# Norm means and prompt steps in the scores' spare PSUM columns, and two attention maps combined with the first map's sum left in

## The chip, the core and the metric

The kernel runs on one core of a Trainium2 chip. The metric is device time of one execution in microseconds. The engines are TensorE (PE; its weight loads are listed as PEld), VectorE (DVE), ScalarE (ACT), GpSimd (POOL) and SyncE (SP), whose queue issues the DMAs. Each engine works through its own list of instructions in order. TensorE reads SBUF and writes PSUM, which has eight banks of 512 float32 columns on 128 partitions; VectorE and ScalarE read PSUM.

## What is computed

One step of a two-layer model on 128 prompt tokens and 1024 sample tokens, width 1024. Each layer makes an input projection, differential attention in four heads, a Fourier branch and a gated spatial branch, and an output projection. The change is in the attention alone. Of the reference:

```python
def _diff_attention(q, k, v, lam, subln_w, lam_init):
    s = jnp.einsum('bhqmd,bhkmd->bhmqk', q, k) * (HEAD_DIM ** -0.5)
    p = jax.nn.softmax(s, axis=-1)
    a = p[:, :, 0] - lam * p[:, :, 1]
    o = jnp.einsum('bhqk,bhke->bhqe', a, v)
    o = o * lax.rsqrt(jnp.mean(jnp.square(o), axis=-1, keepdims=True) + RMS_EPS) * subln_w * (1.0 - lam_init)
    return o
```

The sample tokens attend to 1152 keys (1024 of their own and 128 cached), in blocks of 128 queries; the prompt's 128 tokens attend to themselves. Each head has two maps, m = 0 and 1, and the second is subtracted with the weight lam.

## The kernel before

An attention stage (one per layer) runs 4 heads of 8 blocks of 128 queries. For a block, `score` (lines 632 to 644) multiplies queries and keys of one map into a PSUM tile `S` of three banks, 384 columns of the 512 in each; VectorE takes the negated maximum `nm` (line 640), and ScalarE the exponential `P` with its row sum `zz` (line 642). That is done for both maps. `softmax_diff` (lines 580 to 585) combines them: VectorE takes reciprocals `rz`, GpSimd multiplies the second map by its reciprocal and by minus lam (line 584), and VectorE multiplies the first and adds (line 585). One block later `transpose` (lines 646 to 656) turns the result by nine TensorE transposes into a tile `T`; ScalarE copies it out (line 655) and VectorE takes the remainder `lo` (line 656). For every second block `values` (lines 658 to 665) multiplies by the values into `pv`, squares it on ScalarE, and `finish_o` (lines 592 to 604) takes the mean of the squares over a head's 128 dimensions by a matmul with a matrix of 1/128 (line 594), copies it with epsilon added on ScalarE (`msq`, line 598), and forms the norm by logarithm, exponential and GpSimd products on the gate `gs`.

`S`, `T` and `pv` share the tag `S`: two buffers of three banks each, used in turn, so that each matmul group waits until the group two before it has been read. The other two banks (tag `mm`) serve the projections, whose matmuls (`z`, line 386, and `zt`, lines 401 and 406) fill TensorE between the attention steps. `prompt` (lines 670 to 693) does the prompt's own attention in steps that are stepped on between the others (`side.fill`, paced by `PACE`), with tiles of tag `mm`: two scores `sp`, a transpose `atp`, and the product with its mean, `pvp`.

TensorE's order is the order of the code (`manual_schedule`, line 1059); `attention` (lines 695 to 757) yields between its steps and the loop then issues filler of `FILL[h] * SHARE[step]` ns, 1500 or 1600 per unit in the first three heads and 2950 in the fourth. The order of the other engines is chosen by the scheduler of the framework, from priorities. SBUF tiles share buffers by tag, as the lists `X_TAGS` say: `msq` and `sq` are two of the names in a tag of three buffers, and the prompt's `Pp` is in another.

```python
with tc.manual_schedule(engines={mybir.EngineType.PE}):
    for n, (h, step) in enumerate(attention(l, fill)):
        fill.fill(FILL[h] * SHARE[step])
        if h >= MHEAD:
            extra.fill(MFILL)
```

Of the kernel before, what the change touches and what calls it, by code (L numbers as in the profile page):

```python
# [10 lines left out]
F32 = mybir.dt.float32  # L11
# [20 lines left out]
PACE = 2  # L32
# [19 lines left out]
X_TAGS = {"wr": ("wraw", "woraw", "wada", "tabr", "mr", "ba"), "z": ("zz", "sh", "gt", "vT", "gmt", "gmg", "fot", "vs", "bd", "pqp", "ws", "kc", "vc", "Pp", "modacc"), "Q": ("Q", "bdr", "wsr", "h32"),  # L52
          "sq": ("sq", "wft", "dftp", "msq", "bds", "cb")}
# [9 lines left out]
def backbone_step(ctx, tc, xs, xp, cT, w_ada, b_ada, w_in, w_out, ckT, cv, lamv, wf, wsT, bsT,  # L63
# [60 lines left out]
    mix_d = [dr.tile([128, NT, 6, 128], F32, name=f"mix_{l}") for l in range(L)]  # L124
    neglam = cp.tile([128, L], F32, name="neglam")
# [466 lines left out]
    def finish_o(l, o, ms, sq, n, gs, sl):  # L592

        pe.matmul(ms, lhsT=onesm, rhs=sq[:, :n], start=True, stop=True)
        dve.scalar_tensor_tensor(gs[:, sl], o, subs[:, l:l + 1], gs[:, sl], op0=ALU.mult, op1=ALU.mult)

        m = tX([128, 256], "msq")[:, :n]
        act.activation(m, ms, AF.Identity, bias=epsr)
# [8 lines left out]
    class Head:  # L607
        def __init__(self, l, h):
            self.l, self.h = l, h
            (self.K, self.kp), (self.qr, self.qp) = (res.pop((n, l, h)) for n in "kq")  # L610
# [21 lines left out]
        def score(self, Q, i, m, zz):  # L632
# [3 lines left out]
            for e, q in enumerate((Q[:, m, ql], qlo[i % 2][:, m])):  # L636
                for n in range(3):
                    pe.matmul(S[:, n, :CH], lhsT=q, rhs=K[:, m, n * CH:(n + 1) * CH], start=e == 0, stop=e == 1)  # L638
            nm = small([128, 1], "nm", 4)
# [3 lines left out]
                           accum_out=zz[:, m:m + 1])  # L643
            return P

# [12 lines left out]
        def values(self, p):  # L658
            pv = psS((128, 2, 256), "pv")
            for kt in range(NT):  # L660
                for e, (a, b) in enumerate(((0, 0), (0, 1), (1, 0))):
                    pe.matmul(pv[:, 0, :], lhsT=self.V[:, a, kt, :], rhs=self.A[:, b, kt, :],  # L662
                              start=kt == 0 and e == 0, stop=kt == 8 and e == 2)
            sq = square_o(pv[:, 0], 256)
            return lambda: finish_o(self.l, pv[:, 0], pv[:, 1], sq, 256, self.gs, slice(p * 256, (p + 1) * 256))
# [4 lines left out]
        def prompt(self):  # L670

            l = self.l
            nm = small([128, 2], "nmp", 2)
            zz = small([128, 2], "zzp", 2)
            P = tX([128, 2, 128], "Pp")
            for m in range(2):
                S = psM((128, 128), "sp")
# [476 lines left out]
```

## Time and profile before

| | us |
|---|---|
| median of 3 runs (1438.85 to 1443.56) | 1442.42 |
| profiled execution | 1439.59 |
| its span, first to last instruction | 1437.7 |
| TensorE busy | 1330.9 (93%) |
| VectorE busy | 907.6 (63%) |
| GpSimd busy | 793.4 (55%) |
| ScalarE busy | 746.6 (52%) |
| attention of layer 0 | 90 to 515 |
| attention of layer 1 | 806 to 1240 |

TensorE's busy time is an average over stages; what an edit of the attention is worth is read from the two attention stages, and there from the times in which TensorE waits, with the engine that ended each wait. A wait of another engine matters only if TensorE waits behind it. A time such as "2.24" in a timeline row is from the first start to the last end of the instructions that the row merges.

### The profile page before, as it was taken

To read this page: it belongs to the slowest core of one execution; us is meant where nothing else is said; L and a number is where in the kernel's file an instruction comes from. 1 tells how busy PE (TensorE), PEld (TensorE's weight loads), DVE (VectorE), ACT (ScalarE), POOL (GpSimd) and SP (SyncE) were. 2 spreads that over 40 slices of the span, in tenths; PEclk is the share of its full clock that TensorE was granted. 3 is DMA by queue.
4 is the path that set the end of the run, shared out by engine and by line. 5 is a ranking of instruction groups with operands and counts; after the bars stand their busy time and mean duration, and the time that the engine had idled before them with its cause. 6 is when DMAs were issued, how large, how long until landed. Compare 5 with 4: busy or idle time off the path is not lost. (4 is left out here: it accounts for less than half of the span.)

```text
span 1437.7 us, 21298 instructions
## 1 busy us (share of the span) xinstructions
PE 1330.9 (93%) x8264; PEld 1236.6 (86%) x8264; DVE 907.6 (63%) x1354; ACT 746.6 (52%) x1380; POOL 793.4 (55%) x723
## 2 busy tenths in 40 slices
PE   6899998889899999999997989989799999999997
PEld 4689998879788998987887989988789999998786
DVE  3646667787877865355785565668775684435576
ACT  3576666557454444353656565755565544435320
POOL 2455657567563446336687676575575343533752
PEclk9999999999999999999999999999999999999999
DMA  9310102211220221363341100112020010126432
GB/s 337 147 49 17 35 18 65 75 46 36 88 76 22 98 74 42 108 211 114 124 161 45 50 19 32 49 44 80 32 65 3 30 47 30 47 78 221 154 133 80
DMA packets 56158, 114.43 MB, mean 80 GB/s; under 512 B 4973, under 2 KB 32493, under 8 KB 55929
## 3 DMA queue, kind: packets, MB, share of 16 engines
q1 hardware_dynamic: 56056, 113.07, 23.7%
q8 instruction: 65, 1.06, 0.3%
q14 instruction: 37, 0.30, 0.1%
HBM read 95.47 MB, written 17.58 MB: 79 GB/s over the span
## 5 line engine op out<-in xcount | busy, mean ns | idle before, releaser
L386 PE MATMUL z<-H,w 128*128 128x384 f32 x2520 | 499.8, 345 | 22.4 <-DVE V L506 5.0
L386 PEld LDWEIGHTS z<-H,w 128*128 128x128 f32 x2520 | 444.9, 193 | 29.0 <-ACT vT L492 4.9
L642 ACT ACTIVATE P<-S,nm 128x1152 f32<-128x1152 f32 x128 | 156.4, 1222 | 118.6 <-DVE nm L640 112.1
L640 DVE TENSOR_REDUCE nm<-S 128x1 f32<-128x1152 f32 x128 | 172.3, 1349 | 40.4 <-PE S L638 39.9
L401 PE MATMUL zt<-whi,H 128*128 128x256 f32 x1152 | 158.7, 285 | 4.8 <-ACT ug L767 3.4
L401 PEld LDWEIGHTS zt<-whi,H 128*128 128x128 f32 x1152 | 147.0, 192 | 7.5 <-ACT ug L767 4.0
L584 POOL TENSOR_SCALAR P<-P,rz,neglam 128x1152 f32<-128x1152 f32 x64 | 86.8, 1356 | 98.3 <-DVE rz L583 87.2
L585 DVE SCALAR_TENSOR_TENSOR P<-P,rz 128x1152 f32<-128x1152 f32 x64 | 105.2, 1643 | 42.3 <-POOL P L584 42.3
L630 POOL TENSOR_TENSOR qlo<-qr,Q 64x128 fp32r<-64x128 f32 x128 | 81.4, 641 | 86.8 <-PE S L638 80.2
L367 POOL TENSOR_TENSOR w<-wraw,w 128x1024 fp32r<-128x1024 f32 x36 | 89.6, 2489 | 65.4 <-ACT w L366 64.9
L638 PE MATMUL S<-K,Q 128*128 128x384 f32 x384 | 93.2, 351 | 21.4 <-DVE a L656 11.0
L662 PE MATMUL pv<-a,V 128*128 128x256 f32 x864 | 109.2, 283 | 3.1 <-ACT P L642 3.1
L662 PEld LDWEIGHTS pv<-a,V 128*128 128x128 f32 x864 | 106.6, 191 | 5.1 <-ACT P L642 5.1
L656 DVE TENSOR_TENSOR a<-T,a 128x1152 fp32r<-128x1152 f32 x64 | 86.6, 1353 | 37.5 <-ACT a L655 37.4
L638 PEld LDWEIGHTS S<-K,Q 128*128 128x128 f32 x384 | 67.6, 194 | 29.8 <-DVE a L656 12.8
L638 PE MATMUL S<-K,qlo 128*128 128x384 f32 x384 | 89.7, 342 | 0.0
L1013 PE MATMUL y<-wob,mx 128*128 128x512 f32 (+1 forms) x342 | 88.3, 385 | 1.5 <-DVE rr L1015 1.5
L655 ACT ACTIVATE a<-T 128x1152 fp32r<-128x1152 f32 x64 | 72.3, 1130 | 28.5 <-PE T L652 28.2
L406 PE MATMUL zt<-wlo,H 128*128 128x256 f32 x576 | 82.7, 284 | 1.1 <-POOL wlo L367 1.1
L1013 PE MATMUL y<-wo,mx 128*128 128x512 f32 (+1 forms) x342 | 81.6, 382 | 0.0
L652 PE MATMUL T<-cs,P 128*128 128x128 f32 x576 | 73.9, 274 | 3.8 <-ACT P L642 3.7
L406 PEld LDWEIGHTS zt<-wlo,H 128*128 128x128 f32 x576 | 74.9, 191 | 1.5 <-POOL wlo L367 1.5
(222 smaller groups left out, 2376.9 us busy)
## 6 DMA issues: line engine op xcount, KB each, us to landing
wraw<-in_w_in_dram SPq DMA_DIRECT2D x52, 512.0 KB, 3.3
wada<-in_w_ada_dram SPq DMA_DIRECT2D x32, 512.0 KB, 3.6
wa<-in_w_ada_dram SPq DMA_DIRECT2D x8, 1024.0 KB, 13.0
woraw<-in_w_out_dram SPq DMA_DIRECT2D x16, 512.0 KB, 3.9
mr<-mix SPq DMA_DIRECT2D x18, 384.0 KB, 3.2
mix<-gs SPq DMA_DIRECT2D x8, 576.0 KB, 3.9
x<-rr SPq DMA_DIRECT2D x9, 512.0 KB, 3.6
xr<-x SPq DMA_DIRECT2D x9, 512.0 KB, 5.3
```

The lines of the kernel that those rows point to most:

```text
L367: eng.tensor_tensor(lo, raw, f(hi), op=ALU.subtract)
L386: pe.matmul(z, lhsT=w[:, a, kt, :], rhs=Hc[c][:, b, kt, :], start=n == 0, stop=n == 23)
L401: pe.matmul(z[:, i, :], lhsT=Hc[c][:, a, kt, o:o + 128], rhs=w[0][:, kt, :], start=n == 0, stop=False)
L406: pe.matmul(z[:, i, :], lhsT=Hc[c][:, 0, kt, o:o + 128], rhs=w[1][:, kt, :], start=False, stop=kt == KT - 1)
L584: pool.tensor_scalar(p2, p2, rz[:, 1:2], neglam[:, l:l + 1], op0=ALU.mult, op1=ALU.mult)
L585: return dve.scalar_tensor_tensor(p1, p1, rz[:, 0:1], p2, op0=ALU.mult, op1=ALU.add)
L638: pe.matmul(S[:, n, :CH], lhsT=q, rhs=K[:, m, n * CH:(n + 1) * CH], start=e == 0, stop=e == 1)
L640: dve.tensor_reduce(nm, S[:, :, :CH], axis=AX.XY, op=ALU.max, negate=True)
L642: act.activation(P.rearrange("p (c k) -> p c k", c=3), S[:, :, :CH], AF.Exp, bias=nm, accum_out=zz[:, m:m + 1])
L656: dve.tensor_tensor(lo, T[:, :, 0:3], f(hi), op=ALU.subtract)
L662: pe.matmul(pv[:, 0, :], lhsT=self.V[:, a, kt, :], rhs=self.A[:, b, kt, :], start=kt == 0 and e == 0, stop=kt == 8 and e == 2)
L1013: pe.matmul(z, lhsT=mx[:, a, k, :], rhs=wo[kt][b][:, ns], start=i == 0, stop=i == 23)
```

## The change

Seven things change in the attention, and nothing outside it.

1. The combination of the maps leaves the first map's row sum Z1 in: `softmax_diff_z1` forms P1 + c P2 with c = -lam Z1 / Z2, by a reciprocal of one column, one small VectorE operation and the large one. GpSimd has no part in it. A further small VectorE operation forms e = epsilon Z1 squared for each query.
2. Since the result is too large by Z1, the norm must add e in place of epsilon: the e of two blocks is written to DRAM by a small DMA (4 bytes for each token) and read back on all 128 partitions into `msq`, and VectorE adds the mean to it. ScalarE's copy with epsilon goes for the sample's blocks and stays for the prompt.
3. The mean of the squares is written to the spare columns 384 to 511 of the banks of a later score, in two matmuls of 128 columns: that of a pair of blocks goes into the first map's score of the next even block.
4. The prompt's steps do the same in the second map's scores: the prompt's scores in block 2, its transpose in block 4, its product in block 5, its mean in block 6. They leave the `mm` banks.
5. The reads of the spare columns come behind the score's own exponential. The prompt's two maxima are one instruction.
6. `pv` is one bank part of 256 columns, free once it has been squared and multiplied into the gate, which now happens before the mean.
7. `Pp` moves to the tag of `sq` and `msq`, which keeps its three buffers. The store of a head comes after its last norm, in the next head's block 2.

```diff
+    def softmax_diff_z1(l, p1, p2, zz, ez):
+        c = small([128, 2], "rz")
+        dve.reciprocal(c[:, 0:1], zz[:, 1:2])
+        dve.scalar_tensor_tensor(c[:, 1:2], c[:, 0:1], neglam[:, l:l + 1], zz[:, 0:1], op0=ALU.mult, op1=ALU.mult)
+        dve.scalar_tensor_tensor(p1, p2, c[:, 1:2], p1, op0=ALU.mult, op1=ALU.add)
+        dve.scalar_tensor_tensor(ez, zz[:, 0:1], RMS_EPS, zz[:, 0:1], op0=ALU.mult, op1=ALU.mult)
...
+    def begin_o(l, o, n, gs, sl):
+        sq = square_o(o, n)
         dve.scalar_tensor_tensor(gs[:, sl], o, subs[:, l:l + 1], gs[:, sl], op0=ALU.mult, op1=ALU.mult)
+        return sq
+
+    def mean_o(free, sq, n):
+        for t in range(n // 128):
+            pe.matmul(free[:, t], lhsT=onesm, rhs=sq[:, t * 128:(t + 1) * 128], start=True, stop=True)
+        return free[:, 0:n // 128]
+
+    def finish_o(ms, sq, n, gs, sl, m=None):
+        if m is None:
+            m = tX([128, 256], "msq")[:, :n]
+            act.activation(m.rearrange("p (t k) -> p t k", k=128), ms, AF.Identity, bias=epsr)
+        else:
+            m3 = m.rearrange("p (t k) -> p t k", k=128)
+            dve.tensor_tensor(m3, ms, m3, op=ALU.add)
...
-        def score(self, Q, i, m, zz):
+        def score(self, Q, i, m, zz, aside=None):
...
+            after = aside(S[:, :, CH:]) if aside else None
             nm = small([128, 1], "nm", 4)
             dve.tensor_reduce(nm, S[:, :, :CH], axis=AX.XY, op=ALU.max, negate=True)
...
+            if after:
+                after()
...
         def values(self, p):
-            pv = psS((128, 2, 256), "pv")
+            pv = psS((128, 256), "pv")
...
+            m = tX([128, 256], "msq")
+            sp.dma_start(m, self.e_d[p:p + 1].rearrange("o t q -> o (t q)").partition_broadcast(128))
...
+        def diff(self, i, p1, p2, sums):
+            softmax_diff_z1(self.l, p1, p2, sums[:, i % 2], sums[:, 2, i % 2:i % 2 + 1])
+            if i % 2:
+                sp.dma_start(self.e_d[i // 2].rearrange("t q -> q t"), sums[:, 2])
...
+            return {2: scores, 4: turn, 5: product, 6: norm}
...
-                    p1 = hd.score(Q, i, 0, zz)
+                    p1 = hd.score(Q, i, 0, zz, norm and norm[0])
+                    if norm and norm[1]:
+                        norm[1].store()
...
-                    p2 = hd.score(Q, i, 1, zz)
+                    p2 = hd.score(Q, i, 1, zz, side.get(i))
...
-                    finish = done[0].values(done[1])
-                with tc.high_priority(offset=EARLY):
-                    side.fill(1)
+                    norm = done[0].values(done[1]), done[0] if done[1] == 3 else None
                 yield h, 2
-                with tc.high_priority(offset=EARLY):
-                    finish()
```

How it moves the instructions is shown at three places. In these rows a line number is followed by the operation, by what it writes and reads, and by the shape; numbers after a name tell buffers apart, and x12 is twelve in a row.

The first place is TensorE in the second head of layer 0, at block 4 before and block 2 after, where the prompt's scores stand: S is a score, T the transposes of the block before, z filler, sp and atp the prompt's scores and transpose. Before:

```order
L678 MATMUL sp<-kp,qp_107 128x128
L386 MATMUL z<-H_485,w_1859 128x384 x9
L638 MATMUL S<-K,Q 128x384 x3
L638 MATMUL S<-K,qlo_104 128x384 x3
L678 MATMUL sp<-kp,qp_107 128x128
L386 MATMUL z<-H_485,w_1859 128x384 x6
L638 MATMUL S<-K,Q 128x384 x3
L638 MATMUL S<-K,qlo_104 128x384 x3
L386 MATMUL z<-H_485,w_1859 128x384 x6
L386 MATMUL z<-H_121,w_2115 128x384 x6
L652 MATMUL T<-cs,P 128x128 x9
L685 MATMUL atp<-cs,Pp 128x128
```

And after:

```order
L661 MATMUL S<-K,Q 128x384 x3
L661 MATMUL S<-K,qlo_112 128x384 x3
L716 MATMUL S<-kp,qp_115 128x128 x2
L386 MATMUL z<-H_129,w_1876 128x384 x12
L678 MATMUL T<-cs,P 128x128 x9
L386 MATMUL z<-H_129,w_1876 128x384 x9
L661 MATMUL S<-K,Q 128x384 x3
```

The two prompt scores now stand together behind the second map's score and write into its tile, and the prompt's transpose is no longer in the same block.

The second place is the third head of layer 0, block 2 (326 to 334 us in the trace of before): first VectorE, where nm is a maximum, a the remainder of the transposes, P the combined map, zz the row sums. Before:

```order
L640 TENSOR_REDUCE nm<-S 128x1 x2
L604 SCALAR_TENSOR_TENSOR gs<-msq,gs 128x256
L583 RECIPROCAL rz<-zz_2999 128x2
L417 TENSOR_TENSOR gs<-z,gt 128x384
L656 TENSOR_TENSOR a<-T,a 128x9x128
L585 SCALAR_TENSOR_TENSOR P<-P,rz 128x1152
```

And after:

```order
L664 TENSOR_REDUCE nm<-S 128x1 x2
L620 TENSOR_TENSOR msq<-S,msq 128x256
L593 SCALAR_TENSOR_TENSOR zz_3021<-zz_3021 128x1
L721 TENSOR_REDUCE nmp<-S 128x2
L417 TENSOR_TENSOR gs<-z,gt 128x384
L682 TENSOR_TENSOR a<-T,a 128x9x128
L583 RECIPROCAL rz<-zzp 128x2
L590 RECIPROCAL rz<-zz_3021 128x1
```

The add of the mean (line 620) and the prompt's maximum (line 721), both out of score tiles, now stand between the maxima and the remainder of the transposes. ScalarE at the same place, from the second map's exponential on; K is a part of the keys of the next head. Before:

```order
L642 ACTIVATE P,zz_2999<-S,nm 128x1152
L416 ACTIVATE gt<-gt 128x384
L655 ACTIVATE a<-T 128x9x128
L424 ACTIVATE zz<-z 128x384
L619 ACTIVATE Q<-qr 64x256
```

And after:

```order
L666 ACTIVATE P,zz_3021<-S,nm 128x1152
L416 ACTIVATE gt<-gt 128x384
L621 ACTIVATE sq<-msq 128x256
L681 ACTIVATE a<-T 128x9x128
L723 ACTIVATE Pp,zzp<-S,nmp 128x128 x2
L622 ACTIVATE sq<-sq 128x256
```

The logarithm of the norm (line 621) and the copy of the transposes now stand between the exponential and the prompt's two exponentials (line 723), which read the same tile S.

The third place is ScalarE in block 6 of the second head (273 to 278 us in the trace of before). Before:

```order
L655 ACTIVATE a<-T 128x9x128
L642 ACTIVATE P,zz_2497<-S,nm 128x1152
L492 ACTIVATE vT<-z 128x384
L366 ACTIVATE w_2845<-wraw 128x1024
L187 ACTIVATE wada<-wada,csil 128x1024
```

And after:

```order
L681 ACTIVATE a<-T 128x9x128
L666 ACTIVATE P,zz_2503<-S,nm 128x1152
L492 ACTIVATE vT<-z 128x384
L366 ACTIVATE w_2873<-wraw 128x1024
L617 ACTIVATE msq<-S,epsr 128x128
```

The prompt's mean (line 617), which reads the score's tile S, stands behind a copy and a cast of weights.

## Rows read from the trace of the kernel before

**Rows 1.** Windows: stretch, length, busy time of PE, PEld, DVE, ACT, POOL, clock.

```profile
90.00:515.00 425.00, 391.55 (x2479) 373.65 (x2478) 303.35 (x430) 237.21 (x445) 251.88 (x241) 0.97 0.17 53
...
806.00:1240.00 434.00, 407.28 (x2702) 393.86 (x2701) 287.68 (x422) 246.65 (x462) 244.32 (x243) 0.99 0.12 39
```

**Rows 2.** Waits of PE: who waited for whom, us in total, times, longest.

```profile
PE S L638 <- DVE a L656: 11.0, 3, 4.8
...
PE atp L685 <- DVE rz L583: 6.4, 4, 2.3
PE S L638 <- ACT P L642: 5.2, 4, 1.8
PE S L638 <- ACT msq L598: 5.0, 3, 2.4
...
PE z L386 <- ACT Pp L687: 2.9, 2, 1.5
PE z L386 <- ACT Pp L680: 2.8, 4, 1.2
...
PE atp L685 <- ACT P L642: 2.0, 2, 1.0
```

**Rows 3.** Groups by line and shape: busy us, mean ns of one, idle before.

```profile
L640 DVE TENSOR_REDUCE nm<-S 128x1 f32<-128x1152 f32 x128 | 172.3, 1349 | 40.4 <-PE S L638 39.9
...
L585 DVE SCALAR_TENSOR_TENSOR P<-P,rz 128x1152 f32<-128x1152 f32 x64 | 105.2, 1643 | 42.3 <-POOL P L584 42.3
...
L584 POOL TENSOR_SCALAR P<-P,rz,neglam 128x1152 f32<-128x1152 f32 x64 | 86.8, 1356 | 98.3 <-DVE rz L583 87.2 <-PE T L652 7.5 <-DVE mvv L790 2.8
...
L594 PE MATMUL pv<-sq,cs 128*128 128x256 f32 x64 | 19.1, 379 | 0.0
...
L595 DVE SCALAR_TENSOR_TENSOR gs<-pv,subs,gs 128x256 f32<-128x256 f32 x32 | 15.3, 478 | 15.2 <-PE pv L594 15.2
L598 ACT ACTIVATE msq<-pv,epsr 128x256 f32<-128x256 f32 x32 | 15.2, 474 | 41.5 <-DVE gs L595 41.4
...
L216 DVE SCALAR_TENSOR_TENSOR nb<-mv,rs 128x1 f32<-128x1 f32 x26 | 6.3, 241 | 16.6 <-POOL rs L209 16.4
...
L680 ACT ACTIVATE Pp<-sp,nmp 128x128 f32<-128x128 f32 x16 | 5.8, 360 | 0.0
```

**Rows 4.** Windows, as rows 1: the stretch around the wait at 1022 us.

```profile
1019.00:1027.00 8.00, 4.74 (x17) 4.74 (x18) 6.30 (x5) 3.31 (x7) 2.71 (x3) 0.57 0.22 74
```

**Rows 5.** Timeline, 307 to 314 us: start, length, instructions, idle before.

```profile
307.03 1.31 POOL L584 TENSOR_SCALAR P<-P,rz,neglam 128x1152 f32<-128x1152 f32 x1
...
308.37 3.49 DVE L585 SCALAR_TENSOR_TENSOR P<-P,rz 128x1152 f32<-128x1152 f32 x1 [1.70 <-POOL P L584]
...
311.79 1.34 DVE L656 TENSOR_TENSOR a<-T,a 128x1152 fp32r<-128x1152 f32 x1
...
313.19 1.33 PE L638 MATMUL S<-K,Q 128*128 128x384 f32 x3 [4.76 <-DVE a L656]
```

**Rows 6.** Timeline, third head of layer 0, block 2.

```profile
328.73 2.24 PE L386 MATMUL z<-H,w 128*128 128x384 f32 x12
...
330.81 1.14 PE L652 MATMUL T<-cs,P 128*128 128x128 f32 x9
...
331.49 1.23 ACT L642 ACTIVATE P<-S,nm 128x1152 f32<-128x1152 f32 x1
...
333.12 1.12 ACT L655 ACTIVATE a<-T 128x1152 fp32r<-128x1152 f32 x1
...
333.36 0.68 PE L638 MATMUL S<-K,Q 128*128 128x384 f32 x3
```

**Rows 7.** Timeline, second head of layer 0, block 6: a score, a cast.

```profile
275.94 0.79 PE L638 MATMUL S<-K,Q 128*128 128x384 f32 x3 [0.31 <-ACT P L642]
...
276.15 1.07 ACT L366 ACTIVATE w<-wraw 128x1024 fp32r<-128x1024 f32 x1
```

**Rows 8.** DMA issues: KB each, median us to landing.

```profile
out_new_k_dram<-kp SPq DMA_DIRECT2D x8, 64.0 KB, 1.5
```

More of the change, by code (lines that the diff above doesn't have):

```diff
@@ L124, in backbone_step @@
     mix_d = [dr.tile([128, NT, 6, 128], F32, name=f"mix_{l}") for l in range(L)]
+    e_d = [dr.tile([4, 2, 128], F32, name=f"e_{l}_{h}") for l in range(L) for h in range(H)]
     neglam = cp.tile([128, L], F32, name="neglam")
@@ L670, in prompt @@
         def prompt(self):
[L672 to L677, printed above, removed]
-                pe.matmul(S, lhsT=self.qp[:, m], rhs=self.kp, start=True, stop=True)
-                dve.tensor_reduce(nm[:, m:m + 1], S, axis=AX.X, op=ALU.max, negate=True)
-                act.activation(P[:, m], S, AF.Exp, bias=nm[:, m:m + 1], accum_out=zz[:, m:m + 1])
-                yield 0.5 * PACE
@@ L682, in prompt @@
[L682 to L693 removed]
+            sl = slice(SEQ_S, TOK)
@@ new lines, in scores, with after @@
+            def scores(free):
+                P = self.P = tX([128, 2, 128], "Pp")
+                for m in range(2):
+                    pe.matmul(free[:, m], lhsT=self.qp[:, m], rhs=self.kp, start=True, stop=True)
+                def after():
+                    nm = small([128, 2], "nmp", 2)
+                    zz = small([128, 2], "zzp", 2)
+                    dve.tensor_reduce(nm, free[:, 0:2], axis=AX.X, op=ALU.max, negate=True)
+                    for m in range(2):
+                        act.activation(P[:, m], free[:, m], AF.Exp, bias=nm[:, m:m + 1], accum_out=zz[:, m:m + 1])
+                    softmax_diff(self.l, P[:, 0], P[:, 1], zz, "p")
+                return after
@@ new lines, in turn, with product, after, norm @@
+            def turn(free):
+                pe.transpose(free[:, 0], self.P[:, 0], ident)
+                return lambda: act.activation(self.P[:, 1], free[:, 0], AF.Copy)
+            def product(free):
+                pe.matmul(free[:, 0], lhsT=self.vp, rhs=self.P[:, 1], start=True, stop=True)
+                def after():
+                    self.sq = begin_o(self.l, free[:, 0], 128, self.gs, sl)
+                return after
+            def norm(free):
+                ms = mean_o(free, self.sq, 128)
+                return lambda: finish_o(ms, self.sq, 128, self.gs, sl)
@@ L699, in attention @@
         done = None
-        side = Stream()
+        norm = None
         for n in range(8 * H + 2):
@@ L706, in attention @@
                     hd = Head(l, h)
+                    side = hd.prompt()
                     Qn = hd.pack(0)
@@ L750, in attention @@
                 turn = None
-                with tc.high_priority(offset=EARLY):
-                    side.fill(1)
                 yield h, 3
```

55 lines of the change are left out of this document (20 added, 35 removed).

## The prediction

> **What bounds the kernel now.** I read the windows by stage first, then TensorE's waits, then the groups by line, then three stretches of the timeline. The two attention stages run from 90 to 515 us and from 806 to 1240 us; TensorE is busy 391.55 of 425 us in the first and 407.28 of 434 us in the second [rows 1]. TensorE's order is written out by hand there, and filler matmuls stand between the attention steps, so whatever TensorE waits for cannot be stepped over: the 33.5 and 26.7 us that are left are what this change can win, 60.2 us together, beside what a lowered clock costs after a wait. VectorE is busy 303 of 425 us, 71%: no engine but TensorE is near its limit, but each works in order. The waits by name [rows 2]: score matmuls wait 11.0 us for the eviction of the transposes (DVE a), 5.2 us for exponentials, 5.0 us for the mean's copy (ACT msq); the prompt's transpose waits 6.4 + 2.0 us for the prompt's own softmax, and the filler z waits 2.9 + 2.8 us because the prompt holds its two small PSUM buffers.
>
> **TensorE's own work.** Nothing is dropped: the mean over 256 columns becomes two over 128. A 256-column mean is two passes of 379 ns [rows 3]; nine passes of 128 columns took 1.14 us, 0.127 each [rows 6], so four of them 0.51 us. I take no difference; on either side it is at most 0.2 us at 32 places, 6 us.
>
> **The prompt's and the mean's waits go.** Each of these matmuls now stands behind a score whose inputs are long there: the mean moves past a transpose and about two fillers, the prompt's four steps are two or more blocks apart. 6.4 + 5.0 + 2.9 + 2.8 + 2.0 = 19.1 us [rows 2]. I take all of it; what would be late next at these places is the eviction of the transposes or an exponential, so the lower bound is half, 9.5 us.
>
> **Combining the maps.** 64 GpSimd operations of 1356 ns go, 86.8 us of GpSimd and 42.3 us in which VectorE stood before its own combine [rows 3]. VectorE gets two small operations more per block, priced at the 241 ns of its nearest one-column operation: 128 x 0.241 = 30.8 us; and 32 adds of 256 columns at 478 ns, 15.3 us. So 46.1 us of work replace 42.3 us of standing: VectorE's load in time is even, and what is won is latency. ScalarE loses 32 copies of 474 ns and the 41.4 us that it stood before them [rows 3]. What latency gives on TensorE's path is seen at 307 us [rows 5]: GpSimd's multiply runs from 307.03 to 308.34, the combine runs from 308.37 for 3.49 us, the transposes' eviction ends at 313.13, and a score starts at 313.19 after a wait of 4.8 us. Without the hop the combine can begin one small operation, 0.24 us, after 307.03: 1.1 us earlier. The 3.49 us are 1.85 over its mean of 1.64 [rows 3]; how much of that goes is open, so 1.1 to 2.95 us here. The three waits of 11.0 us have 4.8 as their longest [rows 2], so two are of this size and one is short: 2.5 + 2.5 + 1 = 6 us, between 2.2 and 11.0. The Trainium skill (GPSIMD Engine Reference, section Specifications) says that GpSimd shares its SBUF interfaces with VectorE and contends with instructions of two SBUF inputs; the stretched combine agrees with it, and by that rule the 86.8 us taken off GpSimd would shorten other VectorE work as well, which the sum leaves out.
>
> **What is new: the score's buffer is held longer.** There are two buffers for scores, products and transposes, each used in turn. A score buffer is now free only when the small step in its spare columns has been read too.
> (a) Block 2, where the prompt's scores ride. The nearest stretch is the third head at 326 to 334 us [rows 6]. Before, the exponential of the second map ended at 332.72, the copy of the transposes ran from 333.12 to 334.24, and the next score began at 333.36. Now TensorE does 0.43 us for a mean and 0.43 us for the prompt's scores ahead, so that score is due at 334.2. ScalarE's new order puts a logarithm (taken as the 474 ns of the copy of that size [rows 3]) and the copy of the transposes (1.12 us) before the prompt's two exponentials: 333.12 + 0.47 + 1.12 = 334.7, then two of 360 ns [rows 3], 335.4. The wait is 1.2 to 1.3 us. It is met by three heads in each layer (the fourth has long fillers of weights there): 6 x 1.3 = 7.8 us. Bounds 0 (if ScalarE, without its 41.4 us of standing, is ahead) and 12.
> (b) Block 6, the prompt's mean. ScalarE reads it behind the copy of the transposes, an exponential, a copy and a weight cast. In the second head that cast ends at 277.22 and the score that now needs the buffer started at 275.94 [rows 7]; one read of 0.36 us more makes 277.6: 1.6 us late. Two heads have the cast in front, one has not (0.6 us): 2 x (1.6 + 1.6 + 0.6) = 7.6 us, between 0 and 11.
> (c) The add of the mean on VectorE stands behind the second map's maximum, and the next transposes need that buffer: 1349 + 478 ns = 1.83 us [rows 3] against 2.24 us of filler [rows 6]. It just fits; where VectorE is late by more than 0.4 us TensorE stands. 24 such places, 0 to 0.5 us each: 0 to 12 us, and I take 2, since before this VectorE began a maximum 0.7 us late at most places I looked at.
>
> **The new transfers.** A write of one row sum per token and a broadcast read, 32 of each, on SP's queue. They are two blocks apart, and a block lasts 425 / 32 = 13.3 us [rows 1], against 1.5 us to land for the nearest small write [rows 8]. Behind them on SP stand weight loads, which are issued a block or more ahead of their use. I take 0; where a broadcast waits long for its buffer, a weight load behind it could be late by some us, bounded at 5.
>
> **The clock.** After the 4.8 us wait at 1022 us the granted clock was 0.57 over 8 us [rows 4], the lower of its two levels, 1.2 GHz, for most of it; that is 3.4 us of work. What can come back with this wait and the other removed ones I price at twice this stretch, about 7 us at most; new waits of 1.3 to 1.6 us can bring others. Net 0, between -6 and +6.
>
> **The sum.** -19.1 - 6 + 7.8 + 7.6 + 2 = -7.7 us. Against the profiled execution of 1439.6 us (span 1437.7) that is 1431.9; the median of the runs shown lies 2.8 us above that execution, so 1435 for a median.
>
> **The rivals.**
> 1. *The held buffers decide.* Scores, means and prompt steps share banks, and VectorE and ScalarE read a bank one after the other. The trace has this already: ScalarE stood 41.4 us before the mean's copy, ended by VectorE's multiply out of the same buffer [rows 3]. Place: every head's blocks 2, 4 and 6. Price: (a), (b), (c) at their upper bounds, 12 + 11 + 12, and 6 of clock, 41 us, against 25 removed: +16, about 1458. It decides once the last read of a spare column comes more than about 1.5 us after the score's exponential. For it: ScalarE's new order; against it: that time ScalarE no longer stands. The Trainium skill (PSUM — Partial Sum Buffer, section PSUM bank collisions raise a hardware error) says that no two engines may be on a bank at once, reads included, so the accesses must be put in line; by that rule the maximum of a score also waits for the mean that follows it, and the time would be this rival's. The trace's 41.4 us agrees.
> 2. *It changes places only.* New waits equal the old: 1442, within 4. For it: six of the removed waits stand where new ones appear, in the same heads.
> 3. *Latency carries further.* All 11.0 us for evictions, 5.2 for exponentials, 19.1 and 6 of clock go, and the new waits are halved to 8: -33, about 1410. For it: VectorE's 42.3 us of standing; against it: 46.1 us of new work.
>
> **How the numbers follow.** A measurement tells about 0.3%, 4.3 us, from no change: faster is below 1438.1, slower above 1446.7. Forecast (1427 to 1438) 0.40; rival 3 0.17; rival 2 0.20; rival 1 0.23. So faster 0.57, same 0.20, slower 0.23. The range goes from 1410 to 1453, which leaves out about the lower half of rival 3 and the upper half of rival 1. The forecast's own range is 1427 to 1438.
>
> **What would show it.** Right: no wait of TensorE for the prompt's transpose or for the mean, no idle time of VectorE before the combine; TensorE's idle time in the two stages near 52 instead of 60 us; waits of scores for ScalarE's prompt exponentials and for the prompt's mean. Wrong: waits of transposes for the new add in most blocks (rival 1), waits of the casts for weight loads (the queue), or an idle time near 30 us (rival 3).

## The result and the profile after

The changed kernel takes 1485.12 us (median of 4 runs, 1480.19 to 1490.76) against 1442.43: ratio 1.0317, 95% interval 1.0285 to 1.0348. It is 43 us slower, where 7 us faster was forecast, and it lies above the whole range of 1410 to 1453.

The profiled execution has a span of 1489.0 us against 1437.7. TensorE is busy 1346.0 us instead of 1330.9 and idle 143.0 instead of 106.8: of the 51.3 us, 36.2 are idle time and 15.1 are longer busy time, with a mean granted clock of 0.961 instead of 0.979. The windows tell where. Here the attention is cut from the first to the last score; the columns are stretch, length, and busy time of PE, PEld, DVE, ACT and POOL, then clock, DMA share and GB/s. Before:

```profile
0.00:96.40 96.40, 76.78 (x460) 62.10 (x461) 42.78 (x99) 49.43 (x92) 38.78 (x44) 0.96 0.54 187
96.40:539.90 443.50, 410.05 (x2641) 392.08 (x2640) 319.98 (x444) 246.94 (x459) 259.12 (x243) 0.97 0.17 55
...
807.10:1231.10 424.00, 397.28 (x2624) 383.86 (x2623) 284.14 (x418) 242.62 (x455) 239.66 (x239) 0.99 0.12 39
...
1231.10:1437.70 206.60, 194.24 (x1140) 174.44 (x1138) 113.16 (x166) 71.18 (x120) 93.15 (x70) 0.99 0.36 124
```

And after:

```profile
0.00:101.00 101.00, 77.40 (x460) 63.23 (x461) 42.40 (x99) 49.83 (x92) 38.80 (x44) 0.90 0.51 179
...
101.00:564.70 463.70, 414.50 (x2668) 397.52 (x2667) 343.91 (x517) 240.99 (x447) 206.32 (x213) 0.96 0.22 57
830.60:1273.00 442.40, 403.96 (x2652) 391.48 (x2651) 305.66 (x490) 235.82 (x441) 186.41 (x208) 0.97 0.17 42
...
1273.00:1489.00 216.00, 198.75 (x1143) 177.54 (x1142) 112.70 (x170) 70.01 (x118) 91.16 (x69) 0.97 0.36 119
```

The two attentions are 20.2 and 18.4 us longer, the stretch ahead 4.6 (a clock of 0.90 instead of 0.96) and the end 9.4; the middle is 1.3 shorter. The share of DMA time in the attention rises from 0.17 and 0.12 to 0.22 and 0.17, with hardly more GB/s. The waits of TensorE, who for whom, us in total, times, longest:

```profile
PE T L678 <- DVE msq L620: 25.9, 8, 9.2
PE S L661 <- DVE a L682: 18.5, 12, 3.4
PE S L661 <- ACT P L666: 9.8, 4, 4.4
...
PE T L678 <- DVE gs L603: 6.3, 1, 6.3
PE S L661 <- ACT Pp L723: 5.1, 4, 1.3
...
PE S L661 <- ACT msq L617: 3.9, 2, 3.0
```

Against [rows 2], all that the change was to remove is gone: no wait of the prompt's transpose, none of the filler for the prompt's buffers. The two held buffers of blocks 2 and 6 cost less than forecast, 5.1 and 3.9 us. What came instead stands in the first two rows and in the lone wait of 6.3: the transposes wait for VectorE's add of the mean and for its multiply of the product, and scores wait longer in sum for the eviction by VectorE (18.5 us in 12 waits, where 11.0 in 3 stood). VectorE itself no longer waits to combine: the groups by line (columns as in [rows 3]) have 1.4 us of idle time before line 592, where 42.3 stood.

```profile
L592 DVE SCALAR_TENSOR_TENSOR P<-P,rz 128x1152 f32<-128x1152 f32 x64 | 103.4, 1616 | 1.4
...
L591 DVE SCALAR_TENSOR_TENSOR rz<-rz,neglam,zz 128x1 f32<-128x1 f32 x64 | 25.1, 392 | 1.9
L593 DVE SCALAR_TENSOR_TENSOR zz<-zz 128x1 f32<-128x1 f32 x64 | 24.6, 384 | 12.8 <-ACT P L666 12.1
```

It is late for another reason, which its own waits show:

```profile
DVE macc L190 <- DMA wada<-in_w_ada_dram: 33.8, 12, 8.8
```

Before, this wait was 10.0 us:

```profile
DVE macc L190 <- DMA wada<-in_w_ada_dram: 10.0, 11, 2.7
```

`wada` is a 512 KB piece of the modulation's weights, multiplied by VectorE in between (line 190). The 7.9 us wait at 321 us, one of the longest, followed back in the timeline of the third head of layer 0 (start, length, engine, line, operation, idle before and what ended it):

```profile
294.30 0.38 SPq L704 DMA_DIRECT2D e<-zz  x1
...
302.99 0.33 SPq L691 DMA_DIRECT2D msq<-e  x1
...
303.41 9.01 SPq L181 DMA_DIRECT2D wada<-in_w_ada_dram  x2
...
309.09 1.29 DVE L190 SCALAR_TENSOR_TENSOR macc<-wada,csil,macc 128x1024 f32<-128x1024 f32 x1 [5.36 <-DMA wada<-in_w_ada_dram]
...
311.03 1.89 POOL L430 TENSOR_TENSOR sh<-sh,rp 128x384 f32<-128x384 f32 x1 [6.48 <-DVE sh L429]
...
313.92 2.68 DVE L433 TENSOR_TENSOR qr<-zz,sh 128x384 f32<-128x384 f32 x1 [1.87 <-POOL zz L431]
...
317.07 1.35 DVE L664 TENSOR_REDUCE nm<-S 128x1 f32<-128x1152 f32 x1
...
319.73 1.34 DVE L664 TENSOR_REDUCE nm<-S 128x1 f32<-128x1152 f32 x1
...
321.00 0.41 DVE L620 TENSOR_TENSOR msq<-S,msq 128x256 f32<-128x256 f32 x1
...
321.46 2.18 PE L678 MATMUL T<-cs,P 128*128 128x128 f32 x9 [7.86 <-DVE msq L620]
```

The write of e is issued at 294.30, the read that needs it at 302.99, when the write has landed, and the weights behind it at 303.41; they come at 309.1. VectorE has stood for 5.4 us by then, and the rotation of the queries (lines 429 to 433), both maxima and the add follow behind it in VectorE's order. Both scores of the block had been ready since 311.5, by the same timeline. So the name in the wait, the add, is only the last link. Not all of the delay is the weights': VectorE also waits 1.9 us for GpSimd and spends 2.68 us on a multiply (line 433) beside GpSimd's work, where the same line took 0.54 at 300.54. The page's list of DMAs says how long the new write takes (KB each, median us to landing):

```profile
e<-zz SPq DMA_DIRECT2D x32, 1.0 KB, 8.4
```

8.4 us for 1 KB, and `wada`, which landed in at most 4.4 us before, takes up to 8.5. The first row is from before, the second from after:

```profile
DMA to landing us min/median/max: 3.4/3.6/4.4
...
DMA to landing us min/median/max: 3.4/3.6/8.5
```

### The profile page after: what moved, and what is told of

The parts are those of the page before. It is cut to its first block, busy times and chain, and to the rows that moved or that the text cites. A ratio compares the mean times of both kernels' runs of the same rounds, so it can differ in the third digit from the quotient of the medians.

```text
span 1489.0 us, 21684 instructions
## 1 busy us (share of the span) xinstructions
PE 1346.0 (90%) x8328; PEld 1253.9 (84%) x8328; DVE 948.4 (64%) x1506; ACT 730.5 (49%) x1348; POOL 682.1 (46%) x659
## 4 chain that ended last, share of the span: by engine, by line
PE 37%; DVE 10%; ACT 5%; DMA 4%; issue 3%; POOL 2%; SPq 0%; DVEq 0%; POOLq 0%; ACTq 0%
PE y L1059 9%; PE z L386 8%; PE zt L401 5%; PE S L661 3%; PE pv L688 3%; PE zt L406 3%; DVE nm L664 2%; ACT P L666 2%; PE dft L969 1%; DMA wada<-in_w_ada_dram 1%; PE T L678 1%; DVE rr L1076 1%; DVE rr L1062 1%; DMA wraw<-in_w_in_dram 1%; DVE bns L204 1%
## 5 line engine op out<-in xcount | busy, mean ns | idle before, releaser
L386 PEld LDWEIGHTS z<-H,w 128*128 128x128 f32 x2520 | 447.1, 194 | 18.5 <-DVE V L506 9.1
L652 POOL TENSOR_TENSOR qlo<-qr,Q 64x128 fp32r<-64x128 f32 x128 | 67.4, 531 | 169.9 <-PE S L661 126.8
L661 PE MATMUL S<-K,Q 128*128 128x384 f32 x384 | 94.4, 355 | 37.6 <-DVE a L682 18.5
L678 PE MATMUL T<-cs,P 128*128 128x128 f32 x576 | 78.9, 285 | 32.7 <-DVE msq L620 25.9
L678 PEld LDWEIGHTS T<-cs,P 128*128 128x128 f32 x576 | 69.4, 148 | 37.5 <-DVE msq L620 28.9
L623 POOL TENSOR_TENSOR msq<-msq,sq 128x256 f32<-128x256 f32 (+1 forms) x40 | 32.2, 804 | 139.1 <-ACT sq L622 101.2
L190 DVE SCALAR_TENSOR_TENSOR macc<-wada,csil,macc 128x1024 f32<-128x1024 f32 x44 | 60.8, 1401 | 33.8 <-DMA wada<-in_w_ada_dram 33.8
```

The costliest lines, as they stand in the source:

```text
L386: pe.matmul(z, lhsT=w[:, a, kt, :], rhs=Hc[c][:, b, kt, :], start=n == 0, stop=n == 23)
L678: pe.transpose(T[:, kt // 3, kt % 3, :], a[:, kt * 128:(kt + 1) * 128], ident)
```

## The experiments

Four parts are told apart by a word each: *transfers* (of e), *combine* (the new one), *prompt* (its steps in the spare columns) and *means* (of the sample, in the spare columns). Times are medians; ratios are to the runs of the kernel before on the same chip. That kernel took 1442.43 us beside the changed one and 1438.3 to 1439.5 beside the others, so costs are compared as differences to it. A kernel with the new combine that doesn't use what the transfers bring leaves out Z1 squared: it adds the constant epsilon in place of e, and so stands for the time only. The one with e spread by TensorE is the exception.

### Which part costs

Four kernels take the change apart. The first leaves out the transfers:

```diff
-            sp.dma_start(m, self.e_d[p:p + 1]...partition_broadcast(128))
-                sp.dma_start(self.e_d[i // 2]..., sums[:, 2])
-            dve.tensor_tensor(m3, ms, m3, op=ALU.add)
+            dve.tensor_scalar(m3, ms, RMS_EPS, None, op0=ALU.add)
```

> The changed kernel without its 64 new transfers: the mean is copied out of the spare columns by VectorE with the constant epsilon added (one instruction of the same size), so Z1 squared is left out of the norm's epsilon. Theory 1, the queue (the new transfers wait on SP's queue, 177 us for VectorE's e and 100 us for its landing, and the weight loads behind them come late): 1435 to 1450 us, at least 35 of the 43 us come back, VectorE's idle time before the modulation's multiply for its weights falls from 33.8 us to about the 10.0 us of before. Theory 2, the held score buffers (add of the mean, prompt's reads): over 1470, since all of these reads stay. Theory 3, VectorE's new small operations behind GpSimd: over 1470 too.

1450.64 us, ratio 1.0072 (1.0045 to 1.0098): 11.1 us over the kernel before, so 31.6 of the 42.7 us are back. That is somewhat less than theory 1 expected (at least 35; the time is 0.6 above its range) and far from the others; and it is still slower than before. VectorE's wait for the weights falls as expected, and no piece takes over 4.9 us to land:

```profile
DVE macc L190 <- DMA wada<-in_w_ada_dram: 13.9, 11, 2.0
```

The second was to issue the same transfers later, the write behind the next block's transposes and the read behind `values`:

```diff
-            if i % 2:
-                sp.dma_start(self.e_d[i // 2]..., sums[:, 2])
...
                 yield h, 3
+                if ti % 2 == 1:
+                    th.put(ti // 2)      # the write
...
                 yield h, 2
+                done[0].get()            # the read
```

> The changed kernel with the same 64 transfers, but the write of e is issued one block later and the read one step later, so that both find their input ready more often and SP stands less before them. Theory 1: between 1440 and 1465, SP's waits for VectorE's e fall from 177 us to under 60. Theories 2 and 3: 1480 to 1490, no change.

1478.41 us, 1.0254 (1.0216 to 1.0293). The scheduler put the write nearly where it had been, and SP still waited 191.4 us for e. The reads did move: they are issued 21 to 43 us behind their writes, where the changed kernel issued them 8 to 39 us behind, and SP's waits for a landing (99.9 us) are gone from this trace. That won 3.8 us (38.9 over the kernel before instead of 42.7, and the intervals overlap), so most of the cost doesn't lie in SP's wait for the landing.

The third is combine and transfers alone, on the kernel before:

```diff
-                    softmax_diff(l, p1, p2, zz, "s")
+                    hd.diff(i, p1, p2, sums)      # as in the changed kernel, with the write
...
-        act.activation(m, ms, AF.Identity, bias=epsr)
+        dve.tensor_tensor(m, ms, m, op=ALU.add)       # the sample; m holds the read
```

> The kernel before with the new combine and the transfers alone: VectorE combines without GpSimd, e goes through DRAM and is added by VectorE; the mean stays beside the product and the prompt's steps stay in the two small banks. Theory 1: slower, 1460 to 1485, though no spare column is used. Theory 2: 1430 to 1440, the 6 us of latency of the prediction. Theory 3: 1455 to 1480, with the stretched operations of lines 591 and 593.

1474.32 us, 1.0221 (1.0187 to 1.0255), with VectorE waiting 35.2 us for the weights (13 times, longest 7.8). No spare column is used in it, so the held buffers (rival 1 of the prediction) can't be the main cause.

The fourth is prompt and means with the old combine:

```diff
-            softmax_diff_z1(self.l, p1, p2, sums[:, i % 2], ...)
+            softmax_diff(self.l, p1, p2, sums[:, i % 2], "s")
```

> The changed kernel with the old combine: GpSimd multiplies the second map, ScalarE copies the mean with epsilon, no transfers and no small operations; the mean and the prompt's steps stay in the spare columns. Theory 1: 1430 to 1445 (the prediction's -19 and +17 without the combine). Theory 2: 1465 to 1485. Theory 3: 1430 to 1445, as theory 1.

1443.79 us, 1.0028 (1.0008 to 1.0048): nothing won and little lost, where the prediction's own terms for this part make -1.7 (-19.1 + 17.4).

### Queue or packets

The waits of SP suggest a queue that is held (176.7 us for e, 99.9 for its landing). Three kernels ask. One keeps every transfer and every wait and cuts the size:

```diff
-                sp.dma_start(self.e_d[i // 2]..., sums[:, 2])
+                sp.dma_start(self.e_d[i // 2, :, 0:1]..., sums[0:1, 2])
-            sp.dma_start(m, self.e_d[p:p + 1]...partition_broadcast(128))
+            sp.dma_start(m[0:1, 0:2], self.e_d[p, :, 0:1]...)
```

> The changed kernel with the same 64 transfers at the same places of SP's queue and with the same waits before and behind them, but each moves two numbers of one partition (8 bytes) in place of 256 scattered numbers and a read to 128 partitions; the add of the mean adds the constant epsilon, so Z1 squared is left out. Theory 1a, the waits on the queue hold the weight loads: 1470 to 1488, as the changed kernel. Theory 1b, the many small packets and the 8.4 us that a write takes to land: 1448 to 1460, as without transfers.

1453.99 us, 1.0106 (1.0088 to 1.0125): 3 to 4 us over no transfers, though SP waits for e nearly as long as in the change:

```profile
SPq L704 <- DVE zz L593: 149.6, 20, 24.7
```

So theory 1a falls: these long waits of SP cost nearly nothing. (A wait for a landing of 8 us is not in this run; the kernel with the later reads spoke against it above, and it is told apart below.) The run changes two things at once, the number of pieces and the number of partitions that they come from; no run separates these. The next one moves the full transfers to ScalarE's queue:

```diff
-                sp.dma_start(self.e_d[i // 2]..., sums[:, 2])
+                act.dma_start(self.e_d[i // 2]..., sums[:, 2])
-            sp.dma_start(m, self.e_d[p:p + 1]...partition_broadcast(128))
+            act.dma_start(m, self.e_d[p:p + 1]...partition_broadcast(128))
```

> The changed kernel with its 64 transfers issued by ScalarE in place of SP, so that no weight load stands behind them, while ScalarE's own instructions do. Theory 1a: the loads come in time (VectorE's idle time for wada near 10 us) and the time falls to 1450 to 1470, if ScalarE is held less than SP was. Theory 1b: 1475 to 1490, since the packets are the same. If ScalarE is held for long: above 1490, with TensorE's waits for exponentials much longer.

1493.93 us, 1.0390 (1.0369 to 1.0412): not better, and VectorE still waits 20.4 us for weights (longest 8.0) although no weight load stands behind a transfer in its queue. ScalarE is held too, as the third of the expectations has it, so the time of this run isn't read further. Then the full transfers with nobody using what they bring:

```diff
-            sp.dma_start(m, self.e_d[p:p + 1]...partition_broadcast(128))
+            sp.dma_start(spare, self.e_d[p:p + 1]...partition_broadcast(128))   # spare: in DRAM
-            dve.tensor_tensor(m3, ms, m3, op=ALU.add)
+            dve.tensor_scalar(m3, ms, RMS_EPS, None, op0=ALU.add)
```

> The changed kernel with its 64 transfers at full size and in full number, but nothing waits for what they read: the read goes to a scratch place in DRAM and the add of the mean uses the constant epsilon (Z1 squared is left out). Theory 1b in its first form, the scattered packets make the weight loads behind them land late: 1475 to 1490, with wada landing in 5 us and more at some places. In its second form, the add of the mean waits for its late data: 1450 to 1460.

1494.24 us, 1.0395 (1.0368 to 1.0422); the wait for the weights is 41.6 us, its longest 9.9. So it isn't the add that waits for its data. This run is 13 us slower than the change itself (55.9 us over the kernel before instead of 42.7): its read goes to DRAM and lands in 5.1 us in the median, that of the change goes to SBUF and lands in 3.2.

### The write, the read, or the wait for the landing

Three kernels, each from the one without transfers, with the lines added:

```diff
+                sp.dma_start(self.e_d[i // 2]..., sums[:, 2])                          # write alone
...
+                sp.dma_start(self.e_d[i // 2, :, 0:1]..., sums[0:1, 2])                # read alone
+            sp.dma_start(spare, self.e_d[p:p + 1]...partition_broadcast(128))
...
+                sp.dma_start(self.e_d[i // 2]..., sums[:, 2])                          # write and wait
+            sp.dma_start(spare[0:1, 0:2], self.e_d[p, :, 0:1]...)
```

> The changed kernel with the full write of e (256 numbers of 4 bytes from 128 partitions, 32 times) and no read: nothing on the queue waits for its landing, the add uses the constant epsilon. If the write's packets alone delay the weight loads behind them: 1470 to 1490, wada landing in 5 to 8 us at some places, VectorE's idle time for wada over 25 us. If it is the read, or the wait for the landing: 1450 to 1458.

> The changed kernel with the write of e cut to two numbers of one partition and the full read (1 KB to each of 128 places of a scratch in DRAM, 32 times); the places that it reads are filled once at the start; constant epsilon. If the write is the cause: 1450 to 1460. If the read's 128 packets are: 1470 to 1490.

> The full write of e, and a read of two numbers that waits on SP's queue until the write has landed (8 us), with the weight loads behind it; constant epsilon. If the write's packets are all: as the write alone. If the loads are held by the wait for the landing: 1475 to 1495 here and 1450 to 1458 for the write alone.

Measured: 1478.27 (1.0258, 1.0203 to 1.0313), 1466.34 (1.0191, 1.0138 to 1.0244; in neither of its expected ranges) and 1479.74 (1.0264, 1.0198 to 1.0331). As differences to the kernel before they are 39.0, 27.0 and 40.4 us, against 11.1 without transfers: the write alone costs 27.9 us, waiting for its landing 1.5 more, which is not clear of the noise although SP now stands 251.7 us for the landings, and the read 15.9.

Write and read seem to add up (43.8, and the run with both unused cost 44.8), but the profiled executions speak against reading it so. From the first score to the end of the last, the two attentions together are longer than without transfers by 21.1 us with the write alone, 22.7 with write and wait, 2.1 with the read alone, 44.1 with both unused and 32.1 in the change. So the write costs where the writes stand. The read alone costs next to nothing there; of the 11.0 us that its profiled execution is longer, 9 lie outside, 3.7 ahead of the first score, 4.2 in the middle and 1.1 at the end. Behind a full write a full read costs more than alone; why is open.

In the run with the write alone the late weights can be seen bare, in its timeline:

```profile
289.39 0.38 SPq L703 DMA_DIRECT2D e<-zz  x1
...
293.25 2.47 DVE L190 SCALAR_TENSOR_TENSOR macc<-wada,csil,macc 128x1024 f32<-128x1024 f32 x2
...
295.75 0.33 SPq L181 DMA_DIRECT2D wada<-in_w_ada_dram  x1
...
302.59 1.28 DVE L190 SCALAR_TENSOR_TENSOR macc<-wada,csil,macc 128x1024 f32<-128x1024 f32 x1 [3.71 <-DMA wada<-in_w_ada_dram]
```

Nothing waits for the write here. The weights are issued 6.4 us behind it, when VectorE's multiplies (to 295.72) have freed their buffer, and are there 6.4 us later instead of 3.5. VectorE was free for them at 298.9; at 3.5 us they would have come at 299.3, and it begins at 302.6. It is not one place alone. Of the 18 loads of `wada` whose landing this trace tells, five were issued 4.4 to 8.7 us behind a write, and took 5.2 to 7.9 us; the other 13 took at most 4.4. All five landed 12.3 to 13.9 us after the write's issue, which is 2.3 to 5.5 us after the write's own landing, as if their data had waited for it. What happens inside the DMA engines no trace shows. In the run with ScalarE's queue five loads behind a write took 5.8 to 8.0 us, so the order within one queue isn't the reason. Over the run:

```profile
DVE macc L190 <- DMA wada<-in_w_ada_dram: 26.4, 12, 7.9
```

ScalarE's waits for the input projection's weights grow too, from 7.3 us (longest 1.6) without transfers to 13.0 (longest 7.0). The read alone leaves VectorE's wait at 13.6 us, as without transfers. Its first score comes at 102.7 us instead of 99.0, behind the eight fills at its start, but the kernels that have no fills spread there too, from 96 to 101; the rest of its 15.9 us isn't explained.

### The other three parts, without transfers

Combine alone, on the kernel before:

```diff
-                    softmax_diff(l, p1, p2, zz, "s")
+                    softmax_diff_z1(l, p1, p2, zz, sums[:, 2, i % 2:i % 2 + 1])
```

> The kernel before with the new combine alone, on VectorE, and no transfers: the mean is copied with the constant epsilon by ScalarE as before, so Z1 squared is left out of the norm's epsilon. The prediction's term: -6 us, 1433 or so, between 1429 and 1438. The rival, VectorE has too much in front of TensorE's waits (the changed kernel without transfers took 7 us more than the columns with the old combine): 1443 to 1450. If the transfers are the cause of the 32 us of the run with combine and transfers, this one must lie near 1440 in any case and not above 1452.

1427.74 us, 0.9923 (0.9903 to 0.9942). The prediction's -6 had the right sign; it is -11, a little better than the 1429 to 1438 expected.

Prompt alone, from the run of prompt and means:

```diff
-                    p1 = hd.score(Q, i, 0, zz, norm and norm[0])
+                    p1 = hd.score(Q, i, 0, zz)
                     p2 = hd.score(Q, i, 1, zz, side.get(i))
...
+                pe.matmul(pv[:, 1], lhsT=onesm, rhs=sq, start=True, stop=True)
```

> The kernel before with the prompt's steps alone in the spare columns: old combine, mean beside the product, no transfers. By the prediction's terms: the waits for the prompt's transpose and its two banks go, 6.4 + 2.0 + 2.9 + 2.8 = -14.1, and the held buffers of blocks 2 and 6 come, +13.4 as the run with both columns had them for the prompt's exponentials and +3 for its mean: 1440 to 1446. If the prompt's steps in the scores are the good part: 1430 to 1436.

1420.95 us, 0.9877 (0.9837 to 0.9916). Far better than expected, and better than both kernels; it computes the full norm, so it is the version to keep. Its waits:

```profile
PE T L678 <- ACT P L666: 15.5, 4, 6.0
PE S L661 <- ACT Pp L720: 9.7, 6, 2.9
```

The held buffer of block 2 costs 9.7 us, so the waits that went, 14.1 us in [rows 2], don't by themselves make the 18 us. In the attention the span falls by 10.8 and 7.2 us, TensorE's idle time by 5.8 and 5.1 of it (27.7 and 21.7 us left), the rest is its busy time. This says where they are won, not why: the transposes' waits for exponentials even grew, from 3.7 us to the 15.5 above.

Means alone keeps the first of these lines as the change has it and the prompt's steps as they were before (`side.fill`):

```diff
-                    p1 = hd.score(Q, i, 0, zz)
+                    p1 = hd.score(Q, i, 0, zz, norm and norm[0])
                     p2 = hd.score(Q, i, 1, zz)
```

> The kernel before with the sample's means alone in the spare columns of the next even block's first score: old combine, prompt in its two small banks, no transfers. With both columns the time was 1444, with the prompt's alone 1421, so if the two add up the means in the columns cost 23 us: 1455 to 1465, with the last product of the norm on VectorE in front of the second map's maximum, and a longer end after the last score (202.9 against 198.8 us). If the cost comes only from both together: 1436 to 1444.

1449.99 us, 1.0091 (1.0061 to 1.0121): 12 us lost, about half of what the difference of the two runs with the prompt said, and in neither expected range. Two of its waits:

```profile
PE S L653 <- ACT P L658: 20.9, 6, 5.9
...
PE T L670 <- ACT msq L609: 14.0, 4, 6.6
```

The mean's copy, off the path before but for 5.0 us, now holds a score's buffer, and 14 us of transposes wait for it. And the norm is done a block later, so its last product stands on VectorE between two maxima. The run of prompt and means shows what that can cost. Its timeline:

```profile
147.79 1.34 DVE L664 TENSOR_REDUCE nm<-S 128x1 f32<-128x1152 f32 x1
...
149.79 0.45 POOL L652 TENSOR_TENSOR qlo<-qr,Q 64x128 fp32r<-64x128 f32 x1
149.86 4.41 DVE L626 SCALAR_TENSOR_TENSOR gs<-msq,gs 128x256 f32<-128x256 f32 x1 [0.73 <-POOL msq L624]
150.21 2.39 POOL L367 TENSOR_TENSOR w<-wraw,w 128x1024 fp32r<-128x1024 f32 x1
152.57 0.73 POOL L430 TENSOR_TENSOR sh<-sh,rp 128x256 f32<-128x256 f32 x1
153.26 0.73 POOL L431 TENSOR_TENSOR zz<-zz,rp 128x256 f32<-128x256 f32 x1
...
154.20 1.35 DVE L664 TENSOR_REDUCE nm<-S 128x1 f32<-128x1152 f32 x1
...
155.64 1.22 ACT L666 ACTIVATE P<-S,nm 128x1152 f32<-128x1152 f32 x1 [4.57 <-DVE nm L664]
```

The product of 256 columns lasts 4.41 us in place of 0.4, as long as GpSimd's run of operations beside it; the second map's maximum and exponential come some 4 to 5 us late. How much of the 12 us such places make isn't measured.

Prompt and combine together:

```diff
-            softmax_diff(self.l, p1, p2, sums[:, i % 2], "s")
+            softmax_diff_z1(self.l, p1, p2, sums[:, i % 2], sums[:, 2, i % 2:i % 2 + 1])
```

> The combine on VectorE and the prompt's steps in the spare columns, the mean beside the product as before, no transfers (constant epsilon by ScalarE, so Z1 squared is left out). If the two parts add up, -11 and -18: 1408 to 1414. If both win the same waits: 1418 to 1424.

1434.82 us, 0.9975 (0.9954 to 0.9995). This is above both expected ranges. The two parts don't add: -18 and -11 give -3.5. The waits of scores for the eviction by VectorE are 23.6 us in 12 waits here, against 6.0 in 5 with the prompt alone and 10.2 in 12 with the combine alone. So VectorE comes later to the eviction when both are in; why is left open, no run tells it.

And with e spread by TensorE:

```diff
-                pe.matmul(pv[:, 1], lhsT=onesm, rhs=sq, start=True, stop=True)
+                pe.matmul(pv[:, 1], lhsT=onesm, rhs=sq, start=True, stop=False)
+                for t in range(2):
+                    pe.matmul(pv[:, 1, t * 128:(t + 1) * 128], lhsT=self.ezs[p][:, t:t + 1].to_broadcast([128, 128]),
+                              rhs=identr, start=False, stop=t == 1)
```

> As the run before, but with the full norm: e is spread over the partitions by TensorE, which adds it to the mean in PSUM by a product of e (as a broadcast weight) with the identity, two matmuls of 128 columns for a pair of blocks, 64 in all; no transfer. The two matmuls cost 0.06 to 0.13 us each on TensorE, 4 to 8 us in all: 1412 to 1422 if the parts add up, 1422 to 1432 if not. Under 1421 it beats the prompt's columns alone.

1445.55 us, 1.0047 (1.0025 to 1.0068), 10.7 us more than with the constant and above both expected ranges. (Beyond the lines shown, this kernel also takes the matrix of 1/128 from a single broadcast column.) It takes the transfers' cost away and is still no gain over the kernel before.

The eight cases beside each other, as differences to the kernel before in us:

| parts | us |
|---|---|
| prompt | -18.1 |
| combine | -11.3 |
| prompt, combine | -3.5 |
| prompt, means | +4.3 |
| prompt, means, combine | +11.1 |
| means | +11.7 |
| combine, transfers | +34.8 |
| prompt, means, combine, transfers (the change) | +42.7 |

## Why the prediction was wrong

**The step that failed is "The new transfers": "I take 0 [...] bounded at 5".** They cost 31.6 us in the changed kernel (42.7 - 11.1) and 46.1 on the kernel before (34.8 + 11.3), the write alone 27.9. Two things were wrong in it. The landing was read from a write of 64 KB, 1.5 us in [rows 8], as the nearest small one; but that one moves whole rows. The new write is 256 numbers from 128 partitions, and it took 8.4 us. And the price was looked for in SP's order, in what stands behind a waiting instruction; the queue's waits were there (176.7 us), and cost 3 to 4 us. The cost is in the transfers that run beside the write: the loads of `wada` are issued as VectorE empties one of two buffers and are needed at once. In the trace of before one is issued at 291.34 and multiplied at 295.09, VectorE already waiting for it:

```profile
291.34 7.07 SPq L181 DMA_DIRECT2D wada<-in_w_ada_dram  x2
...
295.09 1.29 DVE L190 SCALAR_TENSOR_TENSOR macc<-wada,csil,macc 128x1024 f32<-128x1024 f32 x1 [0.27 <-DMA wada<-in_w_ada_dram]
```

So the sentence that loads are "issued a block or more ahead of their use" was wrong for them, and a later landing goes straight into VectorE's waits.

The Trainium skill (DMA: Bandwidth & Descriptors, Specifications) gives 512 bytes as the least transfer at line rate, with a read-modify-write below; runs of 4 bytes are far under it, and the trace agrees in direction. Its page SBUF — State Buffer (The DMA setup-cost knee) puts a transfer at about 2 us and its bytes; by that the write would take 2 us, an estimate from the page's figure; the trace has 8.4, and the measurement decides.

**The rest of the sum, point by point.**
- The waits of the prompt and the mean, -19.1: gone from the trace. (The 3.9 us for the prompt's mean are new and counted under (b).) As a gain in time, the prompt's part alone won 18.1, more than its 14.1 of waits less its 9.7 of the held buffer; the mean's share, -5.0, was no gain at all: its columns alone cost 11.7.
- Combining the maps, -6 (2.2 to 11): -11.3 alone. The mechanism was right, VectorE's idle time before the combine is gone. Its two small operations took 25.1 and 24.6 us (lines 591 and 593, means 392 and 384 ns), not 15.4 each at 241 ns. Beside other new work of VectorE it became a loss: 1450.64 with the columns against 1443.79 without it.
- (a), block 2, 7.8 (0 to 12): 5.1 in four waits of 1.3 us. The size of one was right; the first head of each layer has none. The 0.43 us that the working takes for a mean and for the prompt's scores stands in no row; by the 0.127 a pass that the prediction reads from [rows 6] it would be 0.51.
- (b), block 6, 7.6 (0 to 11): 3.9 in two waits.
- (c), the add before the transposes, 2 (0 to 12): 25.9 us with the transfers, 14.9 in 7 waits without. This is the second term that was mis-sized. It was measured against 2.24 us of filler behind a VectorE 0.4 us late; VectorE is later than that wherever the add falls behind other work, at one place of the run without transfers by 4.2.
- The clock, 0 (-6 to 6): TensorE's busy time rose by 15.1 us, by 4.3 in the run without transfers. As after the wait of 4.8 us in [rows 4], the clock is low around the new long waits; around the one of 7.9 us it was 0.66, most of the 15 us at the lower level of 1.2 GHz:

```profile
313.00:328.00 15.00, 7.14 (x30) 6.82 (x29) 12.77 (x13) 8.60 (x15) 11.19 (x10) 0.66 0.21 70
```

**The rivals.** Rival 1, the held buffers, had the right sign, and its sign in the trace is there (transposes that wait for the add); the change without transfers, 11 us over the kernel before, is the most that it can claim, a quarter of the loss, and the new combine has a part in that. Its price, 1458, was the nearest to what came, but by another mechanism. The queue was named among the things that would make the prediction wrong, with too low a bound. Rivals 2 and 3 are out.

## What to carry to other kernels

Don't price a transfer by its kilobytes alone: look at its pieces. Here 1 KB in 4-byte pieces took more than five times as long as 64 KB in rows, and the 512 KB loads issued beside it came late, so first look which loads are used a few us after their issue. A change of several parts with one name can hide a good part behind a bad one: take it apart before dropping it, here 18 us lay in the prompt's steps alone. And gains need not add: here two of 18 and 11 us gave 3.5 together, with longer waits for VectorE.

## What the runs showed of the hardware

- A write of 256 single numbers from 128 partitions to DRAM took 8.4 us in the median (9.0 in the run with the write alone), and 512 KB loads of `wada` issued less than 9 us behind it took 5.2 to 8.6 us instead of 3.5, on the same queue or another; in the kernels without such writes the longest that is known took 5.4.
- A VectorE instruction with two SBUF inputs lasted 4.41 us instead of 0.43 while GpSimd ran two-input operations nearly without a gap, and one of a single column 2.17 us instead of 0.14 (line 593 at 321.33 in the changed kernel, beside GpSimd's 2.35 us from 321.13). In both cases it ended when GpSimd's run did, within 0.3 us. The Trainium skill (GPSIMD Engine Reference, Specifications) names the shared interface and this contention; the trace agrees, with these lengths.
- SP stood 150 us before the small writes at a cost of 3 to 4 us in all, and 252 us for the landings of the full ones at a cost of 1.5 over the write alone.
